# Seven block products for gate and up: a decoder layer's SwiGLU products as 2x2 blocks in seven products, activations and residual through DRAM

## The chip, the cores and the metric

The kernel runs on one core of one Trainium2 chip. The metric is the device time of one execution in microseconds (us). Engines are named as in the profile: PE is TensorE's matrix multiplication and PEld its weight load, DVE is VectorE, ACT is ScalarE, POOL is GpSimd, SP is the queue from which nearly all DMAs are issued.

## The reference

One inference step of a one-layer hybrid decoder, in float32, for 1024 prompt tokens and 8 sequences of 4 sample tokens, so 1056 rows of 1024 features.

```
h = RMSNorm(x) * (1 + scale1) + shift1          # adaLN: mod = SiLU(c) @ w_ada + b_ada
p = h @ w_in                                    # conv inputs, q, k, v
mixer = [short conv (256) | dilated window attention, 3 groups of 4 heads (768)], RMSNorm each
x = x + gate1 * (mixer @ w_out)
h2 = RMSNorm(x) * (1 + scale2) + shift2
x = x + gate2 * ((SiLU(h2 @ w_gate) * (h2 @ w_up)) @ w_down)      # 1024 -> 2816 -> 1024
y = RMSNorm(x) * final_g
```

The sample tokens read caches of keys and values with a T5 relative bias, and the step also returns the caches advanced by four positions, some 26 MB of plain copies.

## The kernel before

Activations lie with features on the 128 partitions and tokens along the free axis, so a product of a weight tile [128 inputs, 128 outputs] with tokens gives one PSUM tile [128 outputs, tokens]. Every large product is made with a high and a low part of both operands (`wh`, `wl` of the weights, `hi`, `lo` of the activations): `mm3` (lines 152 to 159) issues, for each 128 of the inputs, wh·hi (L156), wh·lo (L157) and wl·hi (L158). The splits cost one ACT copy (`wh`, line L89 of the helper `act`) and one DVE subtraction (`wl`, L131) for each weight tile of 128x1024.

Tokens are cut in three blocks, 384, 384 and 288 (`TBS`). The order on each engine is the program's order, with some pieces moved forward by priorities; DMA issues all stand in SP's queue. The stages that matter here:

- Sample bias (`sample_bias`, L898 to L920): for each of the three attention groups the bias rows of the sample tokens are made by eight small matmuls of 32 or 33 rows (L916, L918), 48 in all, from one-hot tables.
- Output projection: `out_pass(tb)` (L1181) runs once for each token block and reads all eight tiles of `w_out` each time, 24 loads and 576 matmuls. Into it are woven the normalisation of the mixer's next block (`mixed`, L1117 on DVE, a copy on ACT, L1121 on POOL or DVE) and the second norm of the block before (`norm2_split`, `split_mod`).
- FFN: `CHUNKS` of 6, 6, 6 and 4 output tiles f. For each f, gate and up are made for three token blocks, 24 matmuls each (3168 in all); SiLU, product and split give `ah` and `al`, which stay in SBUF. After each chunk comes its share of the down projection (1584 matmuls in all), added into the residual `x2` by `add_gated` (L1137).
- Two cache copies are issued behind each f until the 24 are gone. At the end nine `final_rows` normalise and store.

## Time and profile before

| | |
|---|---|
| time, median of 3 runs (range) | 1396.36 us (1395.19 to 1398.0) |
| the profiled execution | 1398.52 us, span 1396.7 us |
| mean granted clock of TensorE | 0.985 of full |
| PE, PEld busy | 1362.6 us (98%), 1253.5 us (90%) |
| DVE, ACT, POOL busy | 561.9, 409.2, 127.6 us |
| DMA | 169.5 MB, mean 121 GB/s |

A row of a timeline or a group gives line, engine, operation, out<-in by the program's names and the shape. Matmuls are pipelined: one of 384 columns shows some 340 ns, while the next starts much earlier, so the pitch from start to start is what a stream of them costs. A stage's busy time that equals its length has no free slot on PE; the difference is waiting.

### The profile page before, as it was taken

The numbers are of one execution on the slowest core, as the hardware profiler recorded it, in microseconds if no ns is written. First come the engines' busy times: TensorE is split into PE (matmuls) and PEld (weight loads), VectorE is DVE, ScalarE is ACT, GpSimd is POOL, SyncE is SP. The second block draws the span as 40 slices with busy tenths as digits, with TensorE's granted clock in tenths as the row PEclk, the third lists the DMA queues.
The fourth block names the chain that finished last, engine by engine and source line by source line (L and its number), as shares of the span: only waits on it lengthen the run. The fifth ranks groups of instructions, "written<-read, shape, count | busy, mean of one in ns | idle before, by whom it ended". The sixth has DMA issues, their size and how long they took to land.

```text
span 1396.7 us, 21319 instructions
## 1 busy us (share of the span) xinstructions
PE 1362.6 (98%) x8810; PEld 1253.5 (90%) x8810; DVE 561.9 (40%) x1160; ACT 409.2 (29%) x853; POOL 127.6 (9%) x139
## 2 busy tenths in 40 slices
PE   8999999999999999999999999999999999999997
PEld 7777667878788978899999999999999999999996
DVE  5722336237216876882222322222322222322266
ACT  5432404242332254662221012221012121112144
POOL 3600000000000055660000000000000000000000
PEclk9999979999899999999999999999999999999998
DMA  9964245128344763561423332222321221111044
GB/s 303 310 240 157 93 141 174 41 81 272 84 144 121 172 183 107 167 228 38 174 98 106 141 107 76 76 69 75 113 76 58 77 64 34 53 46 53 16 145 139
DMA packets 184650, 169.47 MB, mean 121 GB/s; under 512 B 9500, under 2 KB 171807, under 8 KB 184040
## 3 DMA queue, kind: packets, MB, share of 16 engines
q1 hardware_dynamic: 177286, 164.09, 37.1%
q10 hardware_dynamic: 7074, 3.97, 1.1%
q8 instruction: 69, 1.13, 0.3%
q14 instruction: 29, 0.24, 0.0%
q0 software_dynamic: 192, 0.04, 0.0%
HBM read 155.54 MB, written 39.60 MB: 140 GB/s over the span
## 4 chain that ended last, share of the span: by engine, by line
PE 81%; DVE 6%; DMA 6%; issue 2%; ACT 2%; POOL 1%; SPq 1%; DVEq 0%; POOLq 0%; ACTq 0%
PE psmm L156 13%; PE psmm L158 13%; PE psmm L157 13%; PE pss L158 10%; PE pss L156 9%; PE pss L157 9%; PE pss L691 3%; DMA qb<-qs_d 3%; PE pspt L706 2%; PE pso L716 2%; DVE mx L1117 1%; DVE wl L131 1%; PE pso L211 1%; DMA wa<-in_w_ada_dram 1%; DMA wb<-wgt_d 1%
## 5 line engine op out<-in xcount | busy, mean ns | idle before, releaser
L156 PE MATMUL psmm<-hi,wh 128*128 128x384 f32 (+1 forms) x1152 | 378.8, 329 | 1.2 <-DVE ring L1049 0.6
L158 PE MATMUL psmm<-hi,wl 128*128 128x384 f32 (+1 forms) x1152 | 375.9, 326 | 2.1 <-DVE wl L131 2.1
L157 PE MATMUL psmm<-lo,wh 128*128 128x384 f32 (+1 forms) x1152 | 374.6, 325 | 0.0
L89 ACT ACTIVATE wh<-raw 128x1024 fp32r<-128x1024 f32 (+2 forms) x140 | 132.7, 948 | 408.5 <-PE psmm L157 219.5
L156 PEld LDWEIGHTS psmm<-hi,wh 128*128 128x128 f32 x1152 | 217.8, 189 | 17.5 <-issue 12.8
L158 PEld LDWEIGHTS psmm<-hi,wl 128*128 128x128 f32 x1152 | 218.0, 189 | 7.5 <-issue 3.5
L157 PEld LDWEIGHTS psmm<-lo,wh 128*128 128x128 f32 x1152 | 217.8, 189 | 3.4 <-issue 2.9
L131 DVE TENSOR_TENSOR wl<-raw,wh 128x1024 fp32r<-128x1024 f32 (+2 forms) x139 | 155.0, 1115 | 133.7 <-ACT wh L89 132.5
L158 PE MATMUL pss<-hi,wl 128*128 128x384 f32 (+1 forms) x624 | 201.8, 323 | 4.3 <-DVE wl L131 4.3
L156 PE MATMUL pss<-hi,wh 128*128 128x384 f32 (+1 forms) x624 | 202.2, 324 | 0.0
L157 PE MATMUL pss<-lo,wh 128*128 128x384 f32 (+1 forms) x624 | 201.2, 322 | 0.0
L1268 DVE TENSOR_TENSOR sg<-sg,psmm 128x384 f32<-128x384 f32 (+1 forms) x66 | 34.4, 521 | 284.4 <-PE psmm L158 281.3
L158 PEld LDWEIGHTS pss<-hi,wl 128*128 128x128 f32 x624 | 117.8, 189 | 5.9 <-DVE wl L131 5.4
L157 PEld LDWEIGHTS pss<-lo,wh 128*128 128x128 f32 x624 | 117.6, 188 | 1.0 <-issue 0.4
L156 PEld LDWEIGHTS pss<-hi,wh 128*128 128x128 f32 x624 | 117.6, 188 | 0.7
L89 ACT ACTIVATE ah<-sg 128x384 fp32r<-128x384 f32 (+1 forms) x66 | 32.6, 494 | 191.5 <-DVE sg L1268 191.4
L156 PE MATMUL pss<-ah,wh 128*128 128x384 f32 (+1 forms) x264 | 85.4, 323 | 1.1 <-ACT wh L89 1.1
L158 PE MATMUL pss<-ah,wl 128*128 128x384 f32 (+1 forms) x264 | 85.6, 324 | 0.1
L158 PE MATMUL psmm<-ah,wl 128*128 128x384 f32 (+1 forms) x264 | 85.5, 324 | 0.0
L156 PE MATMUL psmm<-ah,wh 128*128 128x384 f32 (+1 forms) x264 | 85.1, 322 | 0.0
L157 PE MATMUL psmm<-al,wh 128*128 128x384 f32 (+1 forms) x264 | 85.1, 322 | 0.0
L157 PE MATMUL pss<-al,wh 128*128 128x384 f32 (+1 forms) x264 | 84.9, 322 | 0.0
(273 smaller groups left out, 1552.4 us busy)
## 6 DMA issues: line engine op xcount, KB each, us to landing
ring<-in_w_ada_dram SPq DMA_DIRECT2D x32, 512.0 KB, 7.0
out_dram<-in_cache_kv_dram SPq DMA_DIRECT2D x8, 2040.0 KB, 8.3
raw<-in_w_in_dram SPq DMA_DIRECT2D x24, 512.0 KB, 4.2
raw<-in_w_out_dram SPq DMA_DIRECT2D x24, 512.0 KB, 4.1
raw<-in_w_gate_dram SPq DMA_DIRECT2D x22, 512.0 KB, 3.9
raw<-in_w_up_dram SPq DMA_DIRECT2D x22, 512.0 KB, 3.8
raw<-in_w_down_dram SPq DMA_DIRECT2D x24, 384.0 KB, 3.5
wa<-in_w_ada_dram SPq DMA_DIRECT2D x32, 256.0 KB, 7.1
```

The lines of the kernel that those rows point to most:

```text
L89: return nc.scalar.activation(out, in_, func, **kw)
L131: nc.vector.tensor_sub(wl[:, :nk], raw[:, :nk], wh[:, :nk].bitcast(F32))
L156: nc.tensor.matmul(out, wh[:, k], h, start=(i == 0), stop=False)
L157: nc.tensor.matmul(out, wh[:, k], l, start=False, stop=False)
L158: last = nc.tensor.matmul(out, wl[:, k], h, start=False, stop=(i == n - 1))
L211: nc.tensor.matmul(psa[32 * j:32 * j + 32, :256], cT[:, k, :], raws[s][:, 256 * j:256 * j + 256], start=(k == 0), stop=(k == KT - 1), tile ...
L691: nc.tensor.matmul(s3[h][:, :nk], q[pr, P * bq:P * bq + P], k[pr, P * kb[0]:P * kb[0] + nk], start=True, stop=True)
L706: nc.tensor.transpose(t4[:, h, j], pt_[:, h, P * j:P * j + P], ident)
L716: nc.tensor.matmul(ops[64 * h:64 * h + 64, :P], vn[:, kb[j], 64 * h:64 * h + 64], ptt[:, h, j], start=(j == 0), stop=(j == nj - 1), tile_p ...
L1117: nc.vector.scalar_tensor_tensor(dst(t[:, sl]), src(x), sv[:, gcol:gcol + 1], dst(rbb[:, sl]), op0=ALU.mult, op1=ALU.mult)
L1268: nc.vector.tensor_mul(sgt[:, :n], sgt[:, :n], ou[:, :n])
```

## The change

Gate and up are made by Strassen's scheme. Tokens are cut in two lanes of 528 and each lane in two quarters of 264; inputs in two halves of 512; outputs in the pairs f and f+11. A product of a 2x2 block of weights with a 2x2 block of activations takes seven block products instead of eight. A block product is 12 matmuls of 264 columns, so one weight (gate or up), one pair and one lane take 84, and all take 3696. The sums and differences that the scheme needs are made on POOL: four of 128x512 for each pair's weights (`weight_units`), four of 128x1056 for each lane's activations (`combos`), and each combination is split anew by ACT and DVE. Three of a lane's partial results are held by ACT copies (`hold`) and the rest is put together on DVE (`put`).

The first two pairs run one lane at a time, which makes eight single-lane products: gate and up of pair 0, gate and up of pair 1 for lane 0, then the same four for lane 1. They are called A to H below, in that order. Pairs 2 to 10 run with both lanes, 18 two-lane products. `norm2(2)` and `norm2(3)` (the second norm for lane 1) and `combos(1)` are issued within A to C.

The gated activations go to DRAM (`a_d`) and come back for the down projection, six tiles a chunk; the residual goes to DRAM before the second norm overwrites it in SBUF, and comes back before the down projection. The output projection runs in two passes of two blocks (272 and 256 columns), with 16 loads of `w_out` and 768 matmuls. The down projection's matmuls are as before. The sample bias is read from the strip of biases in DRAM by 24 small DMAs and a mask. `final_rows` has two output buffers instead of six, and the cache copies stand two behind each product.

```diff
-CHUNKS = ((0, 6), (6, 6), (12, 6), (18, 4))
+NSUB = T // 2
+NQ = NSUB // 2
+FH = DFF // P // 2
+OBS = ((0, 272), (272, 256), (528, 272), (800, 256))
+CHUNKS = ((0, 3), (3, 3), (6, 3), (9, 2))
...
+    a_d = dr.tile([P, 2, FH, T], F32, name="a_d")
...
+    def modulate(tb, x, o, rb):
+        t0, n = OBS[tb]
         n_p = min(n, SEQ - t0)
...
+        for k in range(KT):
+            c = x[:, k, o:o + n_p]
+            nc.vector.scalar_tensor_tensor(c, c, amod[:, 1, k, 0:1], rb[:, :n_p], op0=ALU.mult, op1=ALU.mult)
+            act(c, c, AF.Identity, bias=modt[:, 3, k, 0:1])
...
-    def sample_bias(after):
...
-                for t in range(NT):
-                    rows = slice(32 * t, 32 * t + 32)
-                    nc.tensor.matmul(pbs[rows, :160], rbh.rearrange("k b h -> k (b h)"), ohs[t // 2][:, t % 2],
-                                     start=True, stop=False, tile_position=(0, 32 * t))
-                    nc.tensor.matmul(pbs[rows, :160], sel[:, rows], blk[:, g], start=False, stop=True,
-                                     tile_position=(0, 32 * t))
...
+            h0 = 4 * g * NSTRIP
+            new = ap2.tile([P, NT], F32, tag="sbn", bufs=3, name=nm("sbn"))
+            for t in range(NT):
+                rows = slice(32 * t, 32 * t + 32)
+                at = h0 + (127 - t, 127, 191)[g]
+                n = 64 if g == 2 else P
+                nc.sync.dma_start(bss[g][rows, :n], dram_ap(strip_d, at, [[0, NB], [NSTRIP, 4], [1, n]]))
+                at = h0 + 255 - (t if g == 0 else 0)
+                nc.sync.dma_start(new[rows, :1 if g else NT],
+                                  dram_ap(strip_d, at, [[0, NB], [NSTRIP, 4], [1, 1 if g else NT]]))
...
-    def out_pass(tb, hooks):
-        n = TBS[tb][1]
-        hi, lo = m_hl[tb]
-        for m in range(KT):
-            wh, wl = load_w(w_out_v[:, :, P * m:P * m + P], KT)
-            o = psb()
-            last = mm3(o[:, :n], wh, wl, [(hi[:, k, :n], lo[:, k, :n]) for k in order], order)
-            with tc.high_priority():
-                add_gated(2, m, tb, o)
-            if m in hooks:
-                hooks[m](last)
...
+    def norm2_squares(tb, eng):
+        t0, n = OBS[tb]
+        o = t0 % NSUB
+        acc = squares([(x2[tb // 2][:, k, o:o + n], None) for k in range(KT)], tb, eng)
+        nc.sync.dma_start(xT_d[:, :, t0:t0 + n], x2[tb // 2][:, :, o:o + n])
+        return acc
...
+    def combos(s, pools, tp):
+        h = x2[s]
+        b = [[h[:, 4 * i:4 * i + 4, NQ * j:NQ * j + NQ] for j in range(2)] for i in range(2)]
+        def split(src):
+            pool = pools.pop(0)
+            hi, lo = [pool.tile([P, 4, NQ], F32R, tag="u", bufs=2, name=nm(x)) if pool is w1 else
+                      unit(pool, x, (P, 4, NQ), F32R) for x in ("xh", "xl")]
+            act(hi, src)
+            nc.vector.tensor_sub(lo, src, hi.bitcast(F32))
+            xs[s].append((hi, lo))
+        def diff(p, q):
...
+        t1 = diff(b[0][1], b[0][0])
+        t2 = diff(b[1][1], t1)
+        split(b[0][0])
+        split(b[1][0])
+        split(t2)
+        split(t1)
+        nc.gpsimd.tensor_sub(t2, b[1][0], t2)
+        t3 = diff(b[1][1], b[0][1])
+        split(t3)
+        split(b[1][1])
+        split(t2)
...
+    w_o = [w_out_tile(m) for m in range(2)]
+    last = out_product(w_o[0], 0, 0)
+    mixed_rest(1, acc_m, last)
+    out_product(w_o[1], 1, 0)
+    acc_m = mixed_squares(2)
+    out_product(w_o[0], 0, 1)
+    last = out_product(w_o[1], 1, 1)
+    mixed_rest(2, acc_m, last)
+    for m in range(2, KT):
+        w_o = w_out_tile(m)
+        out_product(w_o, m, 0)
+        last = out_product(w_o, m, 1)
+        if m == 3:
+            sample_merge()
+            acc_m = mixed_squares(3)
+        if m == 5:
+            mixed_rest(3, acc_m, last)
+    acc_2 = [norm2_squares(0, nc.gpsimd), norm2_squares(1, nc.vector)]
     ap2.release()
...
+    sw = tc.alloc_tile_pool(name="sw", bufs=1, side="right", reuse_waits="tile")
+    xb = tc.alloc_tile_pool(name="xb", bufs=1, side="right", reuse_waits="tile")
+    x2[1] = new_x2(xb, 1)
...
+    for m in range(KT):
+        w_o = w_out_tile(m)
+        out_product(w_o, m, 2)
+        last = out_product(w_o, m, 3)
+        if m < 2:
+            norm2(m, acc_2[m], last)
...
+    combos(0, [ua] * 4 + [ub] * 3, xt)
+    acc_2 = [norm2_squares(2, nc.gpsimd), norm2_squares(3, nc.vector)]
...
+    def weight_units(w, f):
+        with tc.high_priority():
+            r1 = load_raw(w[:, :, P * f:P * f + P], KT)
+            r2 = load_raw(w[:, :, P * (f + FH):P * (f + FH) + P], KT)
+        def new(p, q, add=False):
+            t = sw.tile([P, 4, P], F32, tag="sw", bufs=3, name=nm("sw"))
+            (nc.gpsimd.tensor_add if add else nc.gpsimd.tensor_sub)(t, p, q)
+            return t
+        def pair(p, q):
+            wh = wp.tile([P, KT, P], F32R, tag="wh", bufs=2, name=nm("wh"))
+            wl = wp.tile([P, KT, P], F32R, tag="wl", bufs=2, name=nm("wl"))
+            for i, x in enumerate((p, q)):
+                if x is not None:
+                    h = wh[:, 4 * i:4 * i + 4]
+                    act(h, x)
+                    nc.vector.tensor_sub(wl[:, 4 * i:4 * i + 4], x, h.bitcast(F32))
+            return [(wh, wl, 0), (wh, wl, 4)]
+        with tc.high_priority():
+            u = split_raw(r1, KT)
+            yield (*u, 0)
+        yield (*u, 4)
+        with tc.high_priority():
+            s1 = new(r2[:, 0:4], r2[:, 4:8], True)
+            s2 = new(s1, r1[:, 0:4])
+            u = pair(s2, s1)
+        yield from u
+        with tc.high_priority():
+            s3 = new(r1[:, 0:4], r2[:, 0:4])
+            s4 = new(r1[:, 4:8], s2)
+            u = pair(s3, s4)
+        yield from u
+        with tc.high_priority():
+            u = pair(r2[:, 4:8], None)
+        yield u[0]
...
+        for step, bank in enumerate((0, 1, 0, 2, 0, 2, 0)):
+            wh, wl, k0 = next(units)
+            for i, s in enumerate(lanes):
+                o = banks[bank][i][:, :NQ]
+                hi, lo = xs[s][step]
+                for k in range(4):
+                    st = (bank, i) not in started and k == 0
+                    nc.tensor.matmul(o, wh[:, k0 + k], hi[:, k], start=st, stop=False, skip_group_check=True)
+                    nc.tensor.matmul(o, wh[:, k0 + k], lo[:, k], start=False, stop=False, skip_group_check=True)
+                    last = nc.tensor.matmul(o, wl[:, k0 + k], hi[:, k], start=False, stop=(k == 3),
+                                            skip_group_check=True)
+                started.add((bank, i))
+                with tc.high_priority():
+                    if step == 0:
+                        hold(i, "p1", 0)
+                    elif step == 1:
+                        put(i, 0, 0, 1, keep[i, "p1"])
+                    elif step == 2:
+                        hold(i, "u2", 0)
+                    elif step == 3:
+                        hold(i, "p5", 2)
+                    elif step == 4:
+                        put(i, 1, 1, 0, keep[i, "p5"])
+                    elif step == 5:
+                        put(i, 0, 1, 2, keep[i, "u2"])
+                    else:
+                        put(i, 1, 0, 0, None)
...
+    def ffn_pair(f, lanes, pool, bufs, hook=None):
+        sgs = [pool.tile([P, 2, NSUB], F32, tag="sg", bufs=bufs, name=nm("sg")) for _ in lanes]
+        block_product(w_g_v, f, lanes, sgs, False, hook)
+        block_product(w_u_v, f, lanes, sgs, True)
+        for s, sg in zip(lanes, sgs):
+            nc.sync.dma_start(a_d[:, :, f, NSUB * s:NSUB * s + NSUB], sg)
+    def norm2_rest(last):
+        norm2(2, acc_2[0], last)
+        norm2(3, acc_2[1], last)
+    ffn_pair(0, [0], w1, 1, norm2_rest)
+    combos(1, [ua] * 4 + [ub] * 2 + [w1], w1)
+    ffn_pair(1, [0], w1, 1)
+    xb.release()
+    w2 = tc.alloc_tile_pool(name="w2", bufs=1, side="right", reuse_waits="tile")
+    ffn_pair(0, [1], w2, 4)
+    ffn_pair(1, [1], w2, 4)
+    for f in range(2, FH):
+        ffn_pair(f, [0, 1], w2, 4)
...
+    def load_down(f0, nf, m):
+        with tc.high_priority():
+            raw = wp.tile([P, T], F32, tag="raw", bufs=3, name=nm("raw"))
+            r = raw[:, :D].rearrange("p (k c) -> p k c", c=P)
+            for i in range(2):
+                nc.sync.dma_start(r[:, nf * i:nf * i + nf], w_d_v[:, i, f0:f0 + nf, P * m:P * m + P])
+            return split_raw(r, 2 * nf)
...
-            gh, gl = load_w(w_g_v[:, :, P * f:P * f + P], KT)
-            uh, ul = load_w(w_u_v[:, :, P * f:P * f + P], KT)
```

The rows below show three places of the order; their line numbers are those of the kernel they come from.

PE before, at the sample bias (`ohs`, `rbh`, `blk` and `sel` are its tables, `pspt` its bank, `psmm` a product of w_in):

```order
L916 MATMUL pspt_311_1831<-ohs_310_1829,rbh_308_1825 32x160
L918 MATMUL pspt_311_1831<-blk_1823,sel_1821 32x160
L158 MATMUL psmm_335_1914<-hi0_1_94,wl_334_1911 128x384
L156 MATMUL psmm_335_1914<-hi0_1_94,wh_333_1910 128x384
L916 MATMUL pspt_315_1847<-ohs_313_1843,rbh_312_1841 32x160 [waits Activation_49,Pool_49]
L918 MATMUL pspt_315_1847<-blk_1823,sel_1821 32x160
```

PE now, at the same place, behind the last attention products of the first group (`pso`) and at the same w_in product:

```order
L163 MATMUL psmm_336_1905<-hh_1_94,wl_335_1902 128x384
L161 MATMUL psmm_336_1905<-hh_2_95,wh_334_1901 128x384
L704 MATMUL pso_309_1798<-ptt_308_1796,vn_265_1640 64x128 [waits DVE_49,Activation_49]
L704 MATMUL pso_309_1798<-ptt_308_1796,vn_265_1640 64x128 x3
L694 MATMUL pspt_313_1813<-ident_73,p_312_1808 128x128 [waits Activation_49]
L694 MATMUL pspt_313_1813<-ident_73,p_312_1808 128x128
L646 MATMUL pspt_317_1827<-ident_73,ring_222_1270 128x128 [waits PE_49]
L162 MATMUL psmm_336_1905<-hl_10_103,wh_334_1901 128x384
L163 MATMUL psmm_336_1905<-hh_2_95,wl_335_1902 128x384
```

The bias matmuls are gone from PE's order; the product's matmuls stand among those of the attention.

ACT before, in the FFN's third and fourth f (`raw` is a loaded weight tile, `sg` and `ah` the activations of an f):

```order
L89 ACTIVATE wh_1121_6496<-raw_1120_6494 128x1024 [waits DMAHW1_49,PE_49,Activation_49]
L89 ACTIVATE sg_1119_6487<-pss_1117_6437 128x288 [waits PE_49]
L89 ACTIVATE ah_1109_6325<-sg_1119_6487 128x288 [waits DVE_49]
L89 ACTIVATE sg_1130_6558<-pss_1128_6508 128x384 [waits PE_49,Activation_49]
L89 ACTIVATE wh_1124_6502<-raw_1123_6500 128x1024 [waits DMAHW3_49,Activation_49]
L89 ACTIVATE sg_1133_6613<-pss_1131_6563 128x384 [waits PE_49,Activation_49]
L89 ACTIVATE ah_1126_6506<-sg_1130_6558 128x384 [waits DVE_49]
```

ACT now, between the products C and D (`x2_1` is lane 1's residual, `tt` and `xh` a combination of it and its high part, `wh_1181` the first weights of D):

```order
L93 ACTIVATE x2_1_5702<-x2_1_5702,modt_89 128x224 [waits DVE_49] x7
L93 ACTIVATE xh_1144_6652<-tt_1139_6642 128x1056 [waits Pool_49]
L93 ACTIVATE xh_1146_6656<-tt_1138_6640 128x1056
L93 ACTIVATE xh_1153_6671<-tt_1139_6642 128x1056 [waits Pool_49]
L93 ACTIVATE xh_1149_6663<-tt_1148_6661 128x1056 [waits Pool_49]
L93 ACTIVATE xh_1151_6667<-x2_1_5702 128x1056 [waits Activation_49]
L93 ACTIVATE wh_1181_6817<-raw_1179_6813 128x1024 [waits DMAHW6_49,PE_49]
```

D's weights stand behind five copies of lane 1's combinations, three of which wait for POOL; before, a weight copy had only `sg` and `ah` of an earlier f ahead of it.

PE now, at the end of C (`pss_1156`, `psmm_1158` are its banks) and the start of D (`pss_1176`):

```order
L1362 MATMUL psmm_1158_6678<-xh_1073_6264,wh_1172_6757 128x264
L1363 MATMUL psmm_1158_6678<-xl_1074_6265,wh_1172_6757 128x264
L1364 MATMUL psmm_1158_6678<-xh_1073_6264,wl_1173_6758 128x264
L1362 MATMUL pss_1176_6810<-xh_1062_6241,wh_1181_6817 128x264 [waits Activation_49]
L1363 MATMUL pss_1176_6810<-xl_1063_6242,wh_1181_6817 128x264
L1362 MATMUL pspt_1177_6811<-xh_1064_6245,wh_1181_6817 128x264
L1363 MATMUL pspt_1177_6811<-xl_1065_6246,wh_1181_6817 128x264
L1364 MATMUL pss_1176_6810<-xh_1062_6241,wl_1182_6818 128x264 [waits DVE_49]
```

C's sixth block product is followed at once by D's first; C's seventh stands much later, among the products of E.

## Rows read from the trace of the kernel before

**Rows 1.** The page's span, busy times and chain of waits.

```profile
span 1396.7 us, 21319 instructions
...
PE 1362.6 (98%) x8810; PEld 1253.5 (90%) x8810; DVE 561.9 (40%) x1160; ACT 409.2 (29%) x853; POOL 127.6 (9%) x139
...
PE 81%; DVE 6%; DMA 6%; issue 2%; ACT 2%; POOL 1%; SPq 1%; DVEq 0%; POOLq 0%; ACTq 0%
```

**Rows 2.** The core's busy times by stage; the columns are in the first line.

```profile
core 0: us, PE busy (x) PEld busy (x) DVE busy (x) ACT busy (x) POOL busy (x), PEclk, DMA share, GB/s
...
60.00:200.00 140.00, 139.00 (x915) 95.79 (x916) 38.09 (x132) 42.52 (x112) 3.96 (x9) 0.93 0.48 162
...
430.00:640.00 210.00, 198.55 (x1192) 185.90 (x1191) 159.17 (x255) 104.53 (x187) 88.69 (x75) 0.99 0.57 162
640.00:900.00 260.00, 259.98 (x1621) 259.57 (x1621) 68.68 (x114) 45.42 (x73) 0.00 (x0) 1.00 0.32 109
```

**Rows 3.** The timeline of PE in a down projection: start, duration, instruction.

```profile
799.71 0.34 PE L158 MATMUL psmm<-ah,wl 128*128 128x384 f32 x1
...
803.53 0.29 PE L156 MATMUL psmm<-ah,wh 128*128 128x288 f32 x1
...
805.92 0.34 PE L156 MATMUL pss<-ah,wh 128*128 128x384 f32 x1
```

**Rows 4.** Busy times by 5 us around the sample bias, columns as in Rows 2.

```profile
175.00:180.00 5.00, 5.00 (x16) 1.32 (x15) 0.02 (x1) 0.00 (x0) 0.00 (x0) 0.50 0.12 36
...
195.00:200.00 5.00, 5.00 (x37) 4.34 (x36) 1.62 (x3) 0.00 (x0) 0.00 (x0) 1.00 0.66 219
```

**Rows 5.** One group of instructions of PE, by form: count, busy us, mean ns.

```profile
L918 PE MATMUL pspt<-blk,sel 32*32 32x160 f32 x24 | 8.0, 428 | 0.0
```

**Rows 6.** The chain of waits from 172 to 190 us: start, duration, what.

```profile
172.35 0.38 PE pspt L918 x2
...
176.27 0.67 PE pspt L918 x2
...
182.19 0.32 PE psmm L157
```

**Rows 7.** The timeline of the second out projection, start and duration first.

```profile
522.60 1.58 DVE L1117 SCALAR_TENSOR_TENSOR mx<-ring,sv,rbb 128x384 f32<-128x384 f32 x1
524.63 0.60 DVE L1117 SCALAR_TENSOR_TENSOR mx<-ring,sv,rbb 128x384 f32<-128x384 f32 x1
525.16 2.02 DVE L131 TENSOR_TENSOR wl<-raw,wh 128x1024 fp32r<-128x1024 f32 x1
527.23 0.45 PE L158 MATMUL pss<-hi,wl 128*128 128x384 f32 x1 [2.69 <-DVE wl L131]
```

**Rows 8.** Busy times just behind that, columns as in Rows 2.

```profile
525.00:530.00 5.00, 2.77 (x12) 2.77 (x13) 5.00 (x5) 1.62 (x4) 4.05 (x3) 0.87 0.31 91
530.00:535.00 5.00, 5.00 (x24) 5.00 (x24) 3.25 (x4) 3.13 (x5) 3.20 (x3) 0.79 0.27 79
```

**Rows 9.** The groups of ACT, by form: count, busy us, mean ns.

```profile
L89 ACT ACTIVATE wh<-raw 128x1024 fp32r<-128x1024 f32 x92 | 97.2, 1056 | 231.9 <-PE psmm L157 136.1 <-PE pss L157 55.6 <-issue 37.5
...
L89 ACT ACTIVATE wh<-raw 128x512 fp32r<-128x512 f32 x24 | 15.2, 632 | 28.2 <-PE psmm L157 13.3 <-PE pss L157 11.1 <-DMA raw<-in_w_down_dram 2.8
...
L89 ACT ACTIVATE tmp<-tmp,modt 128x256 f32<-128x256 f32 x6 | 3.0, 506 | 1.5 <-DVE tmp L262 1.5
```

**Rows 10.** The same of DVE.

```profile
L131 DVE TENSOR_TENSOR wl<-raw,wh 128x1024 fp32r<-128x1024 f32 x91 | 115.6, 1271 | 119.8 <-ACT wh L89 118.9
...
L131 DVE TENSOR_TENSOR wl<-raw,wh 128x512 fp32r<-128x512 f32 x24 | 16.4, 684 | 4.0 <-ACT wh L89 3.8
...
L1268 DVE TENSOR_TENSOR sg<-sg,psmm 128x288 f32<-128x288 f32 x22 | 10.0, 454 | 28.0 <-PE psmm L158 28.0
```

**Rows 11.** The same of POOL.

```profile
L453 POOL TENSOR_TENSOR xh<-xT,rb 128x384 f32<-128x384 f32 x12 | 11.9, 1017 | 11.8 <-ACT xT L89 10.2 <-DVE rb L366 1.6
```

**Rows 12.** The timeline of the weight loads of eight transposes.

```profile
1367.56 0.91 PEld L1227 LDWEIGHTS pspt<-ident,x 128*128 128x128 f32 x8
```

More of the change, by code (lines that the diff above doesn't have):

```diff
@@ L1215, in hybrid_step, with out_product, w_out_tile @@
-    acc_4 = norm2_squares(2)
+    xa = tc.alloc_tile_pool(name="xa", bufs=1, reuse_waits="tile")
+    x2 = [new_x2(xa, 0), None]
+    def out_product(w, m, tb):
+        t0, n = OBS[tb]
+        o = psb()
+        last = mm3(o[:, :n], *w, [(m_cols(m_hi, tb, k), m_cols(m_lo, tb, k)) for k in order], order)
+        with tc.high_priority():
+            add_gated(2, m, t0, n, x2[tb // 2][:, m, t0 % NSUB:t0 % NSUB + n], o)
+        return last
+    def w_out_tile(m):
+        return load_w(w_out_v[:, :, P * m:P * m + P], KT)
@@ new lines, in block_product, with put, hold @@
+    def block_product(w, f, lanes, sgs, up, hook=None):
+        units = weight_units(w, f)
+        banks = [[ps("s") for _ in lanes], [ps("pt") for _ in lanes], [ps("mm") for _ in lanes]]
+        keep = {}
+        def put(i, row, quarter, bank, other):
+            o = banks[bank][i][:, :NQ]
+            c = sgs[i][:, row, NQ * quarter:NQ * quarter + NQ]
+            if up:
+                if other is not None:
+                    nc.vector.tensor_add(other, o, other)
+                nc.vector.tensor_mul(c, c, o if other is None else other)
+            else:
+                if other is not None:
+                    nc.vector.tensor_add(c, o, other)
+                if hook:
+                    held.append((c, o if other is None else c))
+                else:
+                    silu[0] = act(c, o if other is None else c, AF.Silu)
+        def hold(i, name, bank):
+            if name == "p1":
+                t = w1.tile([P, NQ], F32, tag="p1", bufs=2, name=nm("p1"))
+            else:
+                t = sm.tile([P, 384], F32, tag="tmp", bufs=4, name=nm(name))[:, :NQ]
+            act(t, banks[bank][i][:, :NQ])
+            keep[i, name] = t
+        started = set()
+        for step, bank in enumerate((0, 1, 0, 2, 0, 2, 0)):
+            wh, wl, k0 = next(units)
+            for i, s in enumerate(lanes):
+                o = banks[bank][i][:, :NQ]
+                hi, lo = xs[s][step]
[19 more added lines that the diff above has]
+                        put(i, 0, 1, 2, keep[i, "u2"])
+                    else:
+                        put(i, 1, 0, 0, None)
+            if hook and step == 5:
+                hook(last)
+        with tc.high_priority():
+            for c, o in held:
+                with in_order(last_rstd[0]):
+                    silu[0] = act(c, o, AF.Silu)
+        held.clear()
+        for _ in range(2):
+            if copies:
+                dst, src = copies.pop()
+                with tc.issue_after(last_w[0].ins):
+                    nc.sync.dma_start(dst, src)
@@ L1285, in hybrid_step @@
+    a = load_a(*CHUNKS[0])
+    for m in range(KT):
+        x = (d1 if m < 7 else d2).tile([P, T], F32, tag="x2", bufs=7 if m < 7 else 1, name=nm("x2"))
+        nc.sync.dma_start(x, xT_d[:, m])
+        x2m.append(x)
+    for c, (f0, nf) in enumerate(CHUNKS):
+        if f0 + nf < FH:
+            for m in range(KT):
+                w = load_down(f0, nf, m)
+                for t0, n in TBS:
+                    down(w, a, nf, m, t0, n)
+            a = load_a(*CHUNKS[c + 1])
             continue
-        with tc.issue_after(silu.ins):
+        with in_order(silu[0]):
```

307 lines of the change are left out of this document (125 added, 182 removed).

## The prediction

> **What bounds the kernel now.** I read the page first. PE is busy in 1362.6 of 1396.7 us and holds 81% of the chain of waits [rows 1], so time comes from two places alone: matmuls that go away, and slots on PE that are filled or opened. The table by stage says which stage has such slots. From 640 to 900 us, in gate, up and down, PE has none (259.98 of 260), while DVE is busy for 68.68, ACT for 45.42 and POOL for nothing; from 430 to 640, around the output projection, PE waits for 11.5 us, with DVE at 159 and POOL at 89 [rows 2]. So in the FFN a matmul less is time less, as long as the engines that feed PE keep their slack, and near the output projection they have little. Then the timeline for the price of a matmul: 22 of 384 columns take from 799.71 to 803.53, which is 173.6 ns from start to start, and 18 of 288 columns take to 805.92, which is 132.8 [rows 3]. The difference, 40.8 ns for 96 columns, gives 0.425 ns a column.
>
> **Matmuls of gate and up.** Before, 44 products of (f, weight) with 24 x (173.6 + 173.6 + 132.8) ns = 11.52 us: 506.9 us. Now 3696 matmuls of 264 columns. Going 24 columns below the 288 of the rows gives 132.8 - 24 x 0.425 = 122.6 ns, so 453.1 us, a gain of 53.8. Bounds for the pitch, from the same rows: in proportion to the columns 121.7 ns (a gain of 57), or no shorter than the 132.8 (a gain of 16). I take 122.6, since the two sizes lie on a line and 264 is near. The Trainium skill (TensorE: Matmul & The Clock Gate, Back-to-back issue gap) gives N/2.4 + 2.5 ns, 162.5 and 112.5 for the two sizes here and 112.5 for 264; the trace disagrees by 11 to 20 ns, and by that rule the gain would be 57.
>
> **Sample bias.** Forty-eight matmuls leave PE [rows 5]. This costs more than their number. While they stand in PE's order the granted clock falls to 0.50, though PE is never idle (175 to 180 us), and it is back at 1.00 from 195 [rows 4]. A pair of them takes 0.38 us before the fall and 0.67 after it, and a product's matmul between them 0.32 [rows 6] where 0.174 is normal. The 48 take about 16 x 0.2 + 32 x 0.333 = 14 us; some 8 us of other matmuls at half the clock lose 4. That is 18 at most. Nothing at least: the 24 DMAs are queued on SP behind loads of w_ada that wait for buffers, and the sample scores need them. I take 16, as PE has products of w_in to do meanwhile and 139 of 140 us are busy here [rows 2].
>
> **Output projection.** 576 matmuls in 24 x 8 x 480 ns = 92.2 us become 384 of 272 columns and 384 of 256, at 126.0 and 119.2 ns: 94.2, so 2 more. The mixer's second block now has only three products of PE work to cover its six DVE steps and copies, where it had the rest of a pass. What that does is in the trace: a weight split that stands behind a mixing step made PE wait for 2.69 us, and the clock then fell [rows 7, 8]. Two or three such waits, less the eight loads and splits that go: 5 more, between 0 and 12. Together +7.
>
> **The eight single-lane products.** 84 x 122.6 ns = 10.3 us each, 82 in all, in which ACT, DVE and POOL also do norm2 and both combinations. The durations, by column, from the rows: an ACT copy of 1056 is 1.08 us (1056 ns for 1024) and eight of 224 to 272 with a bias are 4 [rows 9]; a DVE split of 1056 is 1.3 [rows 10]; a POOL sum of 1056 is 2.8 (1017 ns for 384) [rows 11]. The order shows the worst place, between C and D. C's last matmuls there (steps 4 and 5, 3 us) start when their weights are split; eight identities of lane 1's last block (4 us) come behind those weights on ACT; only then can POOL make t1 and t2 (5.6), ACT copy t2 (1.1), DVE subtract (1.3), POOL make the next two (5.6), ACT copy two (2.2), and ACT and DVE split D's first weights (1.1 + 1.3). ACT and DVE take their queues in order, so D's weights, loaded long before, stand behind all of it. 18 us, less what is left of C's steps, and about 2 lost behind it to the clock, as it fell to 0.87 and 0.79 for ten us behind a wait of 2.69 (0.34 x 5 = 1.7) [rows 8]: 19. The other seven boundaries: the next product's first split (1.06 ACT + 1.27 DVE) can begin only when a weight buffer comes free at the end of step 5, and step 6 covers 12 x 122.6 = 1.5 us of its 2.3, so 1 each; A to C and E also share ACT and DVE with norm2 and lane 1's splits, some 11 together. Sum +37, between 15 (C and D overlap better, the rest hidden) and 52.
>
> **The 18 two-lane products.** 20.6 us each. Step 6 is 2.9 us and covers the 2.3. POOL has 4 x 512 columns, 5.4 us, DVE splits of 1.27 + 5 x 0.68 and some ten small results of 0.45 [rows 10], 9 of 20.6 us; ACT less. I take +3, between 0 and 20. What can go wrong is contention: the same mixing step on DVE takes 0.60 us and 1.58, and a split takes 2.02 us against a mean of 1.27, with POOL at work [rows 7, 10]. The Trainium skill (SBUF — State Buffer, Who interferes with whom) says that DVE and POOL take an exclusive lock on a port pair, the loser waiting for the whole instruction; the trace agrees in kind. By that a split would lose up to one POOL instruction, 1.36 us.
>
> **The rest.** At the change to the down projection the first six tiles come back from DRAM, and ACT and DVE split each of them before the weights: +3 (1 to 8). The later chunks' tiles load while the chunk before is multiplied, 8 x 6 x 3 x 480 ns = 69 us. Two output buffers instead of six at the end: +1.5 (0 to 3). The cache copies and the added stores are hidden where DMA is at a share of 0.32 [rows 2]; in the single-lane products they are not, and a late load is in the upper bound there.
>
> **Sum** against the profiled execution: 1398.5 - 53.8 - 16 + 7 + 37 + 3 + 3 + 1.5 = 1380.2. The profiled one is 2.2 above the median, so 1378 for the median.
>
> **Rivals.**
> 1. The stalls are mostly hidden: the scheduler's order lets PE run other products, and the stalls of the pass and the single-lane products come to 18 instead of 42. Time 1354. For it: PE waits for nothing from 640 us on [rows 2]. Against: with one lane there is no other product in PE's order before D.
> 2. Two-lane boundaries lose. If a POOL instruction of 512 (1.36 us) stands in front of the first split at each of the 18 boundaries, with two results on DVE (0.9), the split takes 2.3 + 1.36 + 0.9 = 4.6 against 2.9: 1.65 x 18 = 30, less the 3 counted, so 1405, slower than before. It decides from 1.2 us a boundary on. For it: rows 7. Against: at that time POOL's next sum waits for a buffer that the first splits themselves free.
> 3. A floor under short matmuls. Each of the 4464 matmuls (3696 + 768) needs a weight load; if that holds the pitch at the 132.8 of 288 columns, they cost 10.2 ns more on gate and up and 7 to 14 in the pass, 45 in all: 1423. It decides from 4 ns on. Against: eight loads in a row take 0.91 us, 114 each [rows 12], under 122.6.
> 4. The sample bias brings nothing, its rows being awaited where the matmuls stood: 16 more, 1394.
>
> **Chances.** My forecast 0.62, rival 1 0.17, rival 2 0.09, rival 3 0.05, rival 4 0.07. The likeliest one's own range is 1360 to 1396. No change is within 0.2%, 1393.6 to 1399.2, which is about what a measurement can tell. Faster: 0.60 of the forecast, all of rival 1, half of rival 4 and 0.01 of rival 2, 0.81; within: 0.05; slower: 0.14. The range takes in the hidden stalls and the start of rival 2: 1346 to 1405.
>
> **What would show it.** A pitch of 122 to 124 ns in the two-lane products, and 20.6 to 21 us for each. A granted clock of 1.00 from 170 to 200 us and no matmuls of 32 rows. One wait of PE of 15 us or more for ACT's `wh` at D's start, with a lower clock behind it, and some 80 + 37 us from A to H. If PE's waits there stay under 15 us together, rival 1 is right; if each two-lane product takes 22 us or more, rival 2; if its pitch is over 127 ns, rival 3. I would be wrong altogether if the two passes of the output projection or the down projection's start lost tens of us, which no row here shows.

## The result, and the profile after

The changed kernel takes 1436.03 us (median of four runs, 1431.44 to 1438.84), and the kernel before took 1397.18 beside it: a ratio of 1.0276, with a 95% interval from 1.0244 to 1.0308. The change makes the kernel slower by 2.8%, where the prediction said 1378 us. The profiled execution took 1434.49 us. From its page, the span and the busy times, against [rows 1]:

```profile
span 1432.7 us, 23656 instructions
PE 1323.2 (92%) x9488; PEld 1216.0 (85%) x9488; DVE 719.1 (50%) x1422; ACT 512.5 (36%) x1101; POOL 267.5 (19%) x235
```

PE is busy for 39 us less than before, yet the span is 36 us longer. So the matmuls did go away, and more than their time came back as waiting. Where, the table by stage shows (the kernel after, to be read against [rows 2, 4]; the columns are in its first line):

```profile
core 0: us, PE busy (x) PEld busy (x) DVE busy (x) ACT busy (x) POOL busy (x), PEclk, DMA share, GB/s
175.00:180.00 5.00, 5.00 (x35) 4.34 (x34) 1.95 (x4) 0.00 (x0) 0.00 (x0) 1.00 0.71 225
195.00:200.00 5.00, 5.00 (x37) 4.42 (x36) 2.88 (x6) 1.61 (x3) 0.00 (x0) 1.00 0.97 352
600.00:750.00 150.00, 107.53 (x722) 99.79 (x723) 89.93 (x127) 65.48 (x126) 64.79 (x42) 0.84 0.47 165
750.00:900.00 150.00, 125.00 (x958) 121.43 (x957) 54.92 (x88) 44.58 (x95) 36.99 (x26) 0.93 0.38 135
900.00:1150.00 250.00, 249.73 (x2021) 246.50 (x2020) 121.50 (x198) 98.43 (x197) 63.90 (x46) 1.00 0.28 88
```

The eight single-lane products (600 to 750) and the first five or six two-lane ones (750 to 900) lose 42 and 25 us of PE and part of its clock (0.84 and 0.93 on the mean); from 900 us on PE is full, at 89 us or so for each 720 matmuls. The stages below are cut at the first matmul that reads a combination `xh`, at the first of the last 3024 block matmuls (18 x 168; the products overlap there, so this cut is good to some 0.4 us), and at the first that reads `ah`. In the kernel before, the projection's 24 products run from 503.50 us to the first matmul of gate at 614.30, and the four stretches of gate and up that follow add up to 508.8 us (506.9 by the pitch of [rows 3]).

| stage | forecast, us | measured, us | off by |
|---|---|---|---|
| up to the output projection's first matmul (503.5 before) | 487.5 | 487.9 | +0.4 |
| output projection (110.8 before) | 117.8 | 114.5 | -3.3 |
| single-lane products A to H | 119 | 148.0 | +29 |
| two-lane products | 374 | 405.6 | +32 |
| down projection to the end (273.6 before) | 278.1 | 276.7 | -1.4 |

The five terms leave 56 us; the error of the sum is 54, and the 2 between are what gate and up took before over their pitch. One thing the cut hides: 39 of the projection's matmuls, some 5.5 us, stand behind the first matmul with `xh`, so they count to A to H, in the changed kernel and in all its variants below. Put where they belong, the projection took 120 us (2 over the forecast) and A to H 142.5 (23.5 over). The longest waits of PE in the FFN, from the view of waits (engine, what it ran, what it waited for: total us, count, longest):

```profile
PE pss L1362 <- ACT wh L93: 21.8, 10, 16.1
PE psmm L1362 <- DVE sg L1339: 12.7, 1, 12.7
PE pss L1364 <- DVE wl L136: 11.1, 7, 3.5
PE pss L1362 <- ACT p L93: 7.1, 1, 7.1
PE pspt L1362 <- DVE sg L1339: 3.4, 1, 3.4
```

Each has a place. First D's start on PE, and what ACT did before it (timeline; start, duration, instruction, the idle time before it and its releaser; first PE, then ACT):

```profile
663.72 0.59 PE L1362 MATMUL pss<-xh,wh 128*128 128x264 f32 x1 [16.08 <-ACT wh L93]
```

```profile
658.29 1.08 ACT L93 ACTIVATE xh<-tt 128x1056 fp32r<-128x1056 f32 x1 [3.78 <-POOL tt L1225]
660.67 1.08 ACT L93 ACTIVATE xh<-tt 128x1056 fp32r<-128x1056 f32 x1 [1.29 <-POOL tt L1216]
...
662.63 1.04 ACT L93 ACTIVATE wh<-raw 128x1024 fp32r<-128x1024 f32 x1
```

This is the wait that the prediction worked out: D's weights are the last of the row, behind lane 1's combinations and POOL. The second and third places are not in the prediction. DVE's timeline shows products that cannot be combined, because the buffer `sg` of an earlier pair is still being stored:

```profile
700.99 0.43 DVE L1339 TENSOR_TENSOR sg<-pspt,p 128x264 f32<-128x264 f32 x1 [7.09 <-DMA a_d<-sg]
822.29 0.43 DVE L1339 TENSOR_TENSOR sg<-pspt,p 128x264 f32<-128x264 f32 x1 [4.44 <-DMA a_d<-sg]
849.07 0.43 DVE L1339 TENSOR_TENSOR sg<-pspt,p 128x264 f32<-128x264 f32 x1 [15.26 <-DMA a_d<-sg]
```

And SP's queue, from which those stores are issued (timeline of SP; start, time it took to issue, what):

```profile
811.13 0.37 SPq L124 DMA_DIRECT2D raw<-in_w_gate_dram  x1
811.55 1.21 SPq L1393 DMA_DIRECT2D out_dram<-in_cache_kv_dram  x2
812.80 0.59 SPq L1400 DMA_DIRECT2D a_d<-sg  x1
...
835.26 0.37 SPq L124 DMA_DIRECT2D raw<-in_w_gate_dram  x1
835.68 1.85 SPq L1393 DMA_DIRECT2D out_dram<-in_cache_kv_dram  x3
837.58 0.59 SPq L1400 DMA_DIRECT2D a_d<-sg  x1
```

The store at 837.58 stands behind a weight load that SP could issue only at 835.26, when a buffer `raw` came free, and behind three cache copies. It is the store of pair 1, lane 1 (`sg` has four buffers here, taken in turn), and its data had been complete for 85 us, since the last multiplication of that pair on DVE:

```profile
752.18 0.41 DVE L1336 TENSOR_TENSOR sg<-sg,pss 128x264 f32<-128x264 f32 x1
```

So in SP's order this store stands behind the weight loads and copies of later products. The store's bytes then travel with those of the copies (windows of 5 us of the kernel after, columns as above):

```profile
840.00:845.00 5.00, 0.00 (x0) 0.00 (x0) 0.00 (x0) 0.00 (x0) 0.41 (x1) 0.60 1.15 416
845.00:850.00 5.00, 0.10 (x1) 0.10 (x1) 0.93 (x3) 0.46 (x2) 0.00 (x0) 0.50 0.52 210
```

For most of ten microseconds no engine but the DMA works, and the granted clock falls to 0.60 and 0.50.

### The profile page after: what moved, and what is told of

Read it like the earlier page. It is cut to its first block, busy times and chain, and to the rows that moved or that the text cites. A ratio compares the mean times of both kernels' runs of the same rounds, so it can differ in the third digit from the quotient of the medians.

```text
span 1432.7 us, 23656 instructions
## 1 busy us (share of the span) xinstructions
PE 1323.2 (92%) x9488; PEld 1216.0 (85%) x9488; DVE 719.1 (50%) x1422; ACT 512.5 (36%) x1101; POOL 267.5 (19%) x235
## 5 line engine op out<-in xcount | busy, mean ns | idle before, releaser
L1362 PE MATMUL pss<-xh,wh 128*128 128x264 f32 x704 | 208.0, 298 | 30.8 <-ACT wh L93 21.8
L1364 PE MATMUL pss<-xh,wl 128*128 128x264 f32 x704 | 204.2, 294 | 15.6 <-DVE wl L136 11.1
L1363 PE MATMUL pss<-xl,wh 128*128 128x264 f32 x704 | 202.5, 290 | 0.0
L161 PE MATMUL psmm<-hh,wh 128*128 128x384 f32 (+1 forms) x528 | 177.4, 336 | 0.0
L162 PE MATMUL psmm<-hl,wh 128*128 128x384 f32 (+1 forms) x528 | 174.6, 331 | 0.0
L163 PE MATMUL psmm<-hh,wl 128*128 128x384 f32 (+1 forms) x528 | 174.6, 331 | 0.0
L1362 PEld LDWEIGHTS pss<-xh,wh 128*128 128x128 f32 x704 | 136.7, 194 | 39.4 <-ACT wh L93 26.8
L1364 PEld LDWEIGHTS pss<-xh,wl 128*128 128x128 f32 x704 | 136.2, 194 | 19.2 <-DVE wl L136 13.4
L1363 PEld LDWEIGHTS pss<-xl,wh 128*128 128x128 f32 x704 | 137.1, 195 | 0.0
L1362 PE MATMUL psmm<-xh,wh 128*128 128x264 f32 x352 | 101.1, 287 | 15.6 <-DVE sg L1339 12.7
```

The costliest lines, as they stand in the source:

```text
L161: nc.tensor.matmul(out, wh[:, k], h, start=(i == 0), stop=False)
L162: nc.tensor.matmul(out, wh[:, k], l, start=False, stop=False)
L163: last = nc.tensor.matmul(out, wl[:, k], h, start=False, stop=(i == n - 1))
L1362: nc.tensor.matmul(o, wh[:, k0 + k], hi[:, k], start=st, stop=False, skip_group_check=True)
L1363: nc.tensor.matmul(o, wh[:, k0 + k], lo[:, k], start=False, stop=False, skip_group_check=True)
L1364: last = nc.tensor.matmul(o, wl[:, k0 + k], hi[:, k], start=False, stop=(k == 3), skip_group_check=True)
```

## The experiments

The theory after the result: the work in SP's queue that the prediction called hidden, the cache copies (`out_dram<-in_cache_kv_dram`) and the stores of activations (`a_d<-sg`), costs the 60 us, by its place in the queue or by its bytes. The rivals: the stores alone are at fault, whatever the copies do; or the two-lane boundaries and the single-lane products are simply too full on ACT, DVE and POOL. The stage times of all runs stand together, A to H and two-lane as cut above, each from the profiled execution of its run (A to H with the 5 us or so of the projection's last matmuls):

| kernel | median, us | ratio to before, 95% | A to H, us | two-lane, us |
|---|---|---|---|---|
| changed kernel | 1436.0 | 1.0244 to 1.0308 | 148.0 | 405.6 |
| stores from ACT's queue | 1416.3 | 1.0095 to 1.0162 | 136.4 | 403.2 |
| copies late | 1431.9 | 1.0187 to 1.0263 | 122.9 | 426.1 |
| both | 1435.6 | 1.0231 to 1.0295 | 123.0 | 431.9 |
| before, with bias rows by DMA | 1380.5 | 0.9836 to 0.9934 | | |
| copies from ACT's queue | 1403.7 | 1.0009 to 1.0052 | 146.4 | 377.0 |
| copies in the two-lane part, SP | 1423.1 | 1.0154 to 1.0216 | 122.6 | 416.7 |
| copies in the two-lane part, ACT | 1385.4 | 0.9873 to 0.9943 | 122.7 | 379.4 |
| no copies | 1380.8 | 0.9833 to 0.9905 | 121.5 | 376.4 |
| small copies first | 1430.7 | 1.0198 to 1.0274 | 124.2 | 427.7 |
| three single-lane pairs | 1395.8 | 0.9955 to 0.9991 | 168.1 | 346.0 |

**Stores from ACT's queue.** The edit:

```diff
-            nc.sync.dma_start(a_d[:, :, f, NSUB * s:NSUB * s + NSUB], sg)
+            nc.scalar.dma_start(a_d[:, :, f, NSUB * s:NSUB * s + NSUB], sg)
```

> Only change: the eleven pairs' stores of the gated activations into the DRAM buffer are issued from ScalarE's queue instead of SyncE's. Theory S (the stores stand behind weight loads that wait for buffers, so the buffers of gate results come free late, VectorE's gate additions wait and TensorE runs out of banks): the waits of 7.1, 3.4 and 12.7 us on VectorE's additions and the half clock behind them go, some 30 to 35 us, so 1400 to 1408. Rival C (it is the cache copies' share of the DMA engines that makes weights and stores late, whichever queue issues them): within 8 us of 1436.

Measured 1416.3 us, between the two expectations. The stores now come in time: DVE's waits for them, from its view of waits of the changed kernel and then of this one (total us, count, longest), are

```profile
DVE sg L1339 <- DMA a_d<-sg: 29.7, 4, 15.3
```

```profile
DVE sg L1339 <- DMA a_d<-sg: 1.1, 1, 1.1
```

A to H gained 11.6 us. And yet the two-lane part gained only 2.4. In place of the long waits, ten of 1.56 to 1.91 us stand on PE in its first ten products, from 746.41 to 960.98, 16.4 in all, five for ACT's `wh` and five for DVE's `wl`; these products take 22.6 to 25.3 us, the later ones 20.4 to 20.9. One of the waits on PE, and ACT's timeline at the same place:

```profile
792.45 0.39 PE L1362 MATMUL psmm<-xh,wh 128*128 128x264 f32 x1 [1.56 <-ACT wh L93]
```

```profile
788.46 0.52 ACTq L1400 DMA_DIRECT2D a_d<-sg  x1
790.00 0.42 ACT L93 ACTIVATE sg<-sg 128x264 f32<-128x264 f32 x1 [2.46 <-DVE sg L1339]
791.45 0.42 ACT L93 ACTIVATE sg<-sg 128x264 f32<-128x264 f32 x1 [1.02 <-DVE sg L1339]
791.78 1.66 ACT L93 ACTIVATE wh<-sw 128x512 fp32r<-128x512 f32 x3
```

It isn't the issue of the store, which takes 0.52 us and ends well before. Two silus (`sg<-sg`), which wait for DVE, stand in ACT's order ahead of three weight copies. SP issued its last copies at 988.87 and 1003.29; behind 960.98 no wait is over 0.9 us. In the kernel below with both edits, whose copies start later, nine such waits run from 922.40 to 1112.40. So the stores alone are not at fault: late stores were one way of losing these 25 us, and an order of ACT and DVE that goes with copies on SP is another, which took over; why the planned order goes with them isn't shown.

**Copies late, and both.** The copies are held back to the two-lane products from f = 5 on; the second kernel also has the edit above.

```diff
-            if copies:
+            if copies and f >= 5 and len(lanes) == 2:
```

> Only change: the 24 cache copies start with the sixth pair (two behind each two-lane product) instead of the first. Theory S expects part of the gain only, since the stores still stand behind weight loads, though without copies among them: 1405 to 1425. Rival C expects all of the loss in the two-lane products (33 us over the forecast) and a third of that in the single-lane ones to go: 1390 to 1400.

> Both: stores from ScalarE's queue and copies from the sixth pair on. Theory S: no more than a few us better than the first of this call, 1394 to 1404, with the wait of 16 us between C and D still there. Rival C: like the second of this call within 5 us.

Measured 1431.9 and 1435.6 us, no gain to speak of and above every expectation, and yet half of the theory shows: A to H fell from 148.0 to 122.9, near the 119 forecast. The stall moved. DVE waits for stores again, for 11.5 us up to 1013 and for 5.0 up to 1063. And at the end of the two-lane part there is a new stall; it shows in SP's queue of the first of the two kernels, with DVE's next to last instruction on `sg` and PE behind it:

```profile
1106.55 3.40 SPq L1393 DMA_DIRECT2D out_dram<-in_cache_kv_dram  x4
1131.11 2.04 SPq L1400 DMA_DIRECT2D a_d<-sg  x2
1133.24 1.44 SPq L1449 DMA_DIRECT2D a<-a_d  x2
```

```profile
1130.65 0.43 DVE L1336 TENSOR_TENSOR sg<-sg,pss 128x264 f32<-128x264 f32 x1 [0.57 <-PE pss L1364]
```

```profile
1152.76 0.69 PE L1471 MATMUL pss<-ah,wh 128*128 128x384 f32 x1 [20.68 <-ACT wh L93]
```

The last stores were issued as soon as DVE had made their data, 21 us behind the four copies, which had long landed (the DMA share from 1120 to 1131 us is 0.00). What stands badly are the loads of the down projection (`a<-a_d`): in this order they come behind those last stores, from 1133.24 on, and PE waits 20.68 us for its first weights, which ACT splits behind those tiles. In the changed kernel they are issued 28 us ahead of its last store, which was issued at 1156.59, and PE has no such wait:

```profile
1128.23 20.77 SPq L1449 DMA_DIRECT2D a<-a_d  x6
```

With the stores on ACT as well the wait at this place is 30.5 us, behind the same short waits at boundaries as above; there the loads do stand behind copies, seven from 1128.87 on, and the first is issued at 1136.59. So copies on SP cost in the later place too, but in the first of these kernels by the order that is planned with them and not by a copy's own time.

**The bias rows alone**, in the kernel before:

```diff
-                    nc.tensor.matmul(pbs[rows, :160], rbh.rearrange("k b h -> k (b h)"), ohs[t // 2][:, t % 2],
-                                     start=True, stop=False, tile_position=(0, 32 * t))
-                    nc.tensor.matmul(pbs[rows, :160], sel[:, rows], blk[:, g], start=False, stop=True,
-                                     tile_position=(0, 32 * t))
...
+                nc.sync.dma_start(bss[g][rows, :n], dram_ap(strip_d, at, [[0, NB], [NSTRIP, 4], [1, n]]))
```

> The kernel before with one part of the change alone: the sample bias rows by 24 DMAs instead of 48 matmuls. As the term of the forecast has it: 16 us faster than before, 1381, with the granted clock at 1.00 from 170 to 200 us. Rival (the time comes back in later waits of the sample attention): under 5 us gained, 1392 or more.

Measured 1380.5 us, a gain of 16 by the ratio (0.9885) and 18 by the medians, for the term of 16. The stage of the sample bias of this kernel, against [rows 2]:

```profile
60.00:200.00 140.00, 138.20 (x1003) 105.16 (x1004) 53.64 (x157) 46.57 (x119) 3.81 (x7) 1.00 0.58 198
```

The clock of the stage is 1.00. This part of the change is worth having, and the rest of it cost about 55 us.

**Place against bytes.** Two choices, crossed: copies issued by SP or by ACT, and copies in all products or in the two-lane ones alone (one per product while more than 16 are left, then two). The edits, of which one kernel has the queue, one the place and one both:

```diff
-            if copies:
+            if copies and len(lanes) == 2:
...
-                with tc.issue_after(last_w[0].ins):
-                    nc.sync.dma_start(dst, src)
+                with tc.issue_after(last_a[0].ins):
+                    nc.scalar.dma_start(dst, src)
```

`last_a` is ACT's last copy out of a bank in that product.

> Only change: the cache copies are issued from ScalarE's queue, still two behind each product from the first on, so that none stands between weight loads and stores on SyncE. Theory Q (the place in SyncE's queue is what costs: a store waits behind weight loads and copies, and the order planned around the copies puts D's weights behind lane 1's combinations): most of the 59 us over the forecast from A to the last product goes, 1385 to 1400. Rival C (the copies' transfers themselves crowd the loads and stores): 1420 to 1440.

> Only change: the copies start with the third pair, one behind each two-lane product while the large ones last, then two, all from SyncE as in the changed kernel. Theory Q: the single-lane products as with the late copies (about 124 us instead of 146), stalls of a few us left in the two-lane products, no wait of 20 us before the down projection: 1395 to 1415. Rival C: with at most 8 us of copy in 20.6 us of product no stall is left, 1385 to 1395.

> Copies spread as in the run before and issued from ScalarE's queue. Theory Q and rival C both: the best of the four with copies, 1383 to 1395; if a copy on ScalarE's queue delays its weight splits as the stores did there (1.6 us at a product's boundary), up to 1400.

| A to H + two-lane, us | issued by SP | issued by ACT |
|---|---|---|
| copies in all products | 148.0 + 405.6 | 146.4 + 377.0 |
| copies in the two-lane part | 122.6 + 416.7 | 122.7 + 379.4 |

The two effects stand apart. The single-lane part depends on whether the large copies (2.04 MB each) run there, by 24 to 25 us, and not on the queue. The two-lane part depends on the queue, by 29 to 37 us, and loses little to the bytes: with all of them in it, it takes 379.4 from ACT. The copies on ACT in all products gave 1403.7 us, a little above the range of the view that the place costs and far below that of the bytes. With SP free of copies the store of pair 1, lane 1, that stood for 85 us is issued 0.03 us behind its data (DVE, then SP, copies of all products issued by ACT):

```profile
749.14 0.42 DVE L1337 TENSOR_TENSOR sg<-sg,pss 128x264 f32<-128x264 f32 x1
749.59 0.53 SPq L1401 DMA_DIRECT2D a_d<-sg  x1
```

In this kernel the windows of the two parts are:

```profile
602.00:748.00 146.00, 105.50 (x712) 98.40 (x713) 85.65 (x120) 63.57 (x125) 61.44 (x41) 0.85 0.74 248
748.00:1125.00 377.00, 373.37 (x3030) 369.12 (x3028) 180.89 (x292) 144.55 (x296) 98.56 (x71) 1.00 0.29 91
```

and in the first of them POOL waits for a weight tile (timeline of POOL):

```profile
677.44 1.26 POOL L1293 TENSOR_TENSOR sw<-raw 128x512 f32<-128x512 f32 x1 [14.17 <-DMA raw<-in_w_gate_dram]
```

The DMA share is 0.74 and POOL loses 14 us on one weight load. SP had issued that load at 663.29, so its place in the queue is not what held it: it came 14 us later, where such loads land after 3.9 us in the kernel before (median), while two copies that ACT had issued at 659.32 and 663.94 travelled and the DMA share was 1.00 and 0.96 (660 to 670 us). The wait of 16 us for D's weights is not there; the longest of PE is 9.49, for a combination `xh` that ACT copied at 681.12. So the loss of 24 us has not one form: in the changed kernel its largest wait comes from an order in which D's weights stand last, here from other places, with this late load among them. The order that the scheduler plans differs between the two, and moving copies moves it; how much of the 24 us is order and how much bytes stays open. Copies in the two-lane part by ACT give 1385.4 us, as both views expected, and 0.9% faster than before (0.9908). With copies there by SP, 1423.1, which met neither of its expectations, the stores are late again (two issued at 894.60 and 895.24 had their data at 859.3 and 863.2), and PE waits 14.2 us at the start of the down projection.

**No copies.** The test of the whole theory.

```diff
-        for _ in range(2):
+        for _ in range(0):
```

> The changed kernel without the 24 cache copies (their outputs are left unwritten): what is left is the scheme alone. Both theories: 1385 to 1395; what it lacks to the forecast without stalls (1398.5 - 54 - 16 + 2 = 1331 for the profiled execution) is then not the copies' doing.

Measured 1380.8 us, a little under its expectation. The two parts, in the windows of this kernel:

```profile
600.00:725.00 125.00, 101.42 (x720) 95.63 (x719) 98.61 (x128) 64.94 (x126) 70.88 (x43) 0.93 0.33 101
725.00:1102.00 377.00, 374.74 (x3029) 369.52 (x3027) 182.40 (x291) 147.20 (x296) 98.17 (x71) 1.00 0.26 82
```

121.5 and 376.4 us stand against the forecast's 119 and 374, and by the same cuts each of the other three stages lies within 2 us of its forecast. The sum is right without copies, but not by the forecast's way: ACT's timeline has D's weights ahead of the combinations, not behind them.

```profile
654.56 1.04 ACT L93 ACTIVATE wh<-raw 128x1024 fp32r<-128x1024 f32 x1
661.03 1.08 ACT L93 ACTIVATE xh<-tt 128x1056 fp32r<-128x1056 f32 x1 [5.11 <-POOL tt L1216]
```

No wait of PE there is over 4.2 us. The 39 us over the 82 of matmuls are some 5 of the projection's last matmuls, many short waits, with DVE busy for 98.6 of 125 us, and a clock of 0.93.

**Small copies first.** The large copies leave the single-lane part, with the queue and the number of copies as they were:

```diff
-                dst, src = copies.pop()
+                dst, src = copies.pop(0)
```

> The changed kernel with the cache copies in the opposite order: the eight of 248 KB fall into the single-lane products, the eight of 1016 KB and the eight of 2040 KB into the two-lane ones; all from SyncE as before. If the bytes copied decide the single-lane part (theory T, from the runs with copies off SyncE, which still took 146 us there), it shrinks from 148 to 122 to 130 us while the two-lane part stays at 400 us or more, about 1405 to 1420. If the place in the queue alone decides it there too, it stays at 140 or more and the time at 1425 or more.

A to H came to 124.2, as expected of the bytes; the two-lane part rose to 427.7, so the whole, 1430.7, is above what was expected: with the large copies now there, DVE waits for stores five times, 40.0 us in all, against four times and 29.7 in the changed kernel.

**Three pairs in single lane**, on the kernel of 1385.4 us, to see whether short cover at the change from C to D, or the amount of work of the other engines, makes the 40 us of A to H:

```diff
     ffn_pair(1, [0], w1, 1)
+    ffn_pair(2, [0], w1, 1)
...
     ffn_pair(1, [1], w2, 4)
-    for f in range(2, FH):
+    ffn_pair(2, [1], w2, 4)
+    for f in range(3, FH):
```

> The spread copies from ScalarE's queue, and three pairs run one lane at a time instead of two, so that lane 0 has six products before lane 1 is needed. If the 40 us still lost in the single-lane products are lane 1's preparation waiting for cover, they shrink to 25 or less and the time falls to 1370 to 1378. If VectorE is what is full there (splits, results, norm and combinations), the loss stays and four boundaries of a single lane come on top: 1386 to 1394.

Measured 1395.8 us, a little above the range for a full DVE. The twelve products take 168.1 us, 44.5 over their matmuls, where eight were 40 over. But the edit put no matmul among lane 1's preparation. Cut at every 84th matmul, the first four products take 18.3, 14.4, 18.2 and 22.8 us here and 18.3, 14.4, 18.3 and 22.4 in the kernel of 1385.4, which is 32 of the 40 us; and ACT makes the last `xh` of lane 1 69 us behind the first block matmul in both. So the loss is where the second norm and lane 1's combinations run, and the pair added stands behind them. That work of the other engines (DVE above all, with 98.6 of 125 us) limits this part is likely and not shown; whether that preparation would be hidden under more matmuls stays untested.

## Why the prediction was wrong

- **Pitch of the matmuls: right.** Neighbouring two-lane products start at 888.87 and 909.52, from the timeline of PE:

```profile
888.87 0.29 PE L1362 MATMUL pspt<-xh,wh 128*128 128x264 f32 x1
...
909.52 0.29 PE L1362 MATMUL pspt<-xh,wh 128*128 128x264 f32 x1
```

  20.65 us for 168 matmuls is 122.9 ns, against 122.6. The 53 us are there, and the rival of a floor at 132.8 ns is out. By the rule of the Trainium skill (TensorE: Matmul & The Clock Gate, Back-to-back issue gap) 288 columns take 122.5 ns, where the prediction's text has 112.5, and 264 take 112.5; the trace is 10.3 and 10.4 above it. The section gives that rule for a single matmul and says that in a stream of weight loads and matmuls, as here, both set the spacing.
- **Sample bias: right**, 15.6 us for 16 in the changed kernel and 16 to 18 alone, with the clock at 1.00 from 175 to 180 us where it had been 0.50 [rows 4]. The rival that it brings nothing is out.
- **Output projection and the end: right in size**, some +9 for +7 (120 us with the matmuls that stand in A's stretch, against 110.8), and +3 for +4.5 behind it (276.7 against 273.6).
- **Single-lane products: the step named happened, and others were left out or too small.** The wait at D, put at 15 to 18 us, was 16.08, and another 3.53 followed at half the clock. That the size was met has some luck in it: the steps that the prediction lists for this wait add up to 22 us, less 3 for C's last steps, where it wrote 18. The rest came from the buffer `sg`, from short waits, and from the clock, 0.84 on the mean from 600 to 750 us, where the prediction counted 2 us for it. The late load that the prediction kept for its upper bound doesn't show in this kernel: POOL's longest wait for a weight tile there is 4.3 us, and 4.9 in the kernel of 1385.4. In lane 0 `w1` has one such buffer, so the next pair waits for its store. The store was issued at 695.49, though its data was complete at 645.5, and PE's matmul behind it started at 701.90 after a wait of 7.07 us. A wait for a store was nowhere in the sum. Rival 1, that the scheduler hides most of this, needed less than 15 us of waits and is out.
- **Two-lane products: the failed step.** "The cache copies and the added stores are hidden where DMA is at a share of 0.32" took a mean share for an answer on order. Nothing in that share says when a store is issued in a queue that also holds loads waiting for buffers. The store of pair 1, lane 1, was issued 85 us after its data, and the third and fourth two-lane products took 27.7 and 38.4 us where the undisturbed ones take 20.4 to 21.2, some 25 us lost. Taking the copies off SP's queue, with nothing else, gave back 28.6 us of the 32 (405.6 to 377.0), and the stores are then issued with their data. Taking the stores off it ended DVE's waits for them (29.7 us to 1.1), but gave back 2.4, as the order of silus and weight copies on ACT made up for it; why the planned order goes with the copies' queue stays open. Rival 2 also put the loss at the two-lane boundaries, by POOL and DVE; in the undisturbed part PE is busy 249.73 of 250 us, so that mechanism is out.
- **The range** ended at 1405 with rival 2. It held no case of a queue, though the prediction itself let the sample bias's DMAs stand behind waiting loads on the same SP.

The forecast of 1378 is thus near the time of the kernel without copies, 1380.8, and of the kernel with copies by ACT, 1385.4. Also then the scheme gains nothing that these runs can show: the bias rows alone in the kernel before give 1380.5, and the intervals overlap. The 53 us of matmuls are spent again, in the kernel of 1385.4 on A to H (40, the projection's last matmuls among them), the projection ahead of that (3), the two-lane products over their matmuls (8) and the down projection (4).

## What to carry to other kernels

A store whose buffer is needed again is on the critical path by its place in the issuing queue: list what stands before it there, loads that wait for buffers and bulk copies above all, and price that, whatever the mean DMA share says. Bulk copies belong on a queue that holds no waiting load and no store that work waits for, and in a stage in which PE has weights ahead. Where fewer matmuls are bought with more work on other engines, the stage that has least cover pays first, and its loss can take most of the gain (here some 35 to 40 of 53 us).

## What the runs showed of the hardware that was not expected

- SP's queue is served in order also where its instructions are ready at different times: the store issued at 837.58 had its data from 752.59 on and held up DVE by 15.26 us, and the kernel with the copies on ACT's queue has no such wait.
- Issuing a DMA from ACT was cheap here: 0.52 us for a store of 528 KB, and with all 24 copies issued by ACT in the two-lane part this took 379.4 us, against 376.4 with none.
- Waits cost twice. The clock fell to 0.50, the lower of its two levels, within the 16.08 us wait and was still there behind it, from 665 to 670 us (windows of 5 us of the kernel after; columns as above), where matmuls start 0.22 us apart and not 0.12. In the first 150 us of the FFN it was 0.84 on the mean.

```profile
650.00:655.00 5.00, 0.00 (x0) 0.00 (x0) 1.43 (x2) 2.06 (x2) 2.50 (x2) 0.50 0.49 209
665.00:670.00 5.00, 1.50 (x7) 1.50 (x8) 3.45 (x2) 0.00 (x0) 2.37 (x2) 0.50 0.02 3
```
